# A gated linear recurrence on TensorE: two levels in one row of products, and half the query columns in the next four

## The chip, the cores and the metric

The kernel runs on one core of one Trainium2 chip. The metric is device microseconds of one execution. TensorE (PE in the profile; PEld is its weight load) multiplies a stationary operand of up to 128 columns with a streamed operand and writes to PSUM; VectorE (DVE) and ScalarE (ACT) do elementwise work; GpSimd (POOL) does small things here; SyncE (SP) issues the weight transfers.

## The reference

Two decoder layers on 256 tokens of width 1024, float32. A layer normalises x, projects it by `h @ w_in` into ten groups of 512 columns, runs three branches side by side, multiplies their outputs by silu(gate), projects by `w_out` and adds x:

- MoBA attention, 8 heads of 64 (with 256 tokens there is one block, so it is causal attention over the block);
- HGRN2, a gated linear recurrence, 4 heads with key and value width 128;
- attention to 256 memory tokens, 4 heads of 128.

The change is in the recurrence. For a head, with query q_t (after silu), key k_s, value v_s and a forget gate f_t per key channel, the reference computes, chunk by chunk,

```
scores[t, s] = sum_d q[t, d] * (f[s+1, d] * ... * f[t, d]) * k[s, d]     for s <= t
o[t] = sum_s scores[t, s] * v[s]
```

and then a per-head RMS norm of o.

## The kernel before, in words

**Projections.** The weights come in chunks of 128 x 1024. For each chunk ScalarE makes a rounded copy `wh` (L144, L147) and VectorE the remainder `wl` (L156, L159); TensorE multiplies them in three passes with the split activations (L196, `acc`; the output projection is L1051). These projections are most of TensorE's work. The chunks are loaded five ahead, `wh` is made three ahead and `wl` two ahead.

**The order.** The stream of projections is cut into slots of a few multiplies. In each slot the function `step` gives every active generator (one for each side job: the recurrence, a branch, a transposition) one turn; `yield n` means that the generator sits out n slots. So the side jobs' instructions are laid between the projections. PSUM has four side tiles (`sd`) beside the four accumulators; `room("sd")` waits for one to be free. After that a scheduler of the language orders each engine's instructions by its own simulated times; the recurrence's products go through `mm_row`, which keeps them in the program's order.

**The recurrence (g_hgrn, L711 to L808).** Q, K and F hold queries, keys and gates as [key channel 128, head 4 x token 256], 1024 columns. The products of gates are never formed for every pair (s, t). Instead there are levels m = 0, 1, 2, 4, ..., 64, then a last one over halves of 128:

- At level m the pairs are those whose s lies in an even run of m tokens and t in the odd run behind it (m = 0: s = t). By then each Q in an odd run has been multiplied by the gates from its run's start to t, and each K in an even run by the gates from behind s to its run's end, so a plain product K^T Q over key channels gives the scores of these pairs.
- For m below 32 (L729 to L733) TensorE computes, for each of the 32 blocks of 32 tokens (8 halves of heads i, 4 blocks j in each), the whole 32 x 32 product: 32 key columns are loaded, 32 query columns are streamed, and the result goes to partitions 32j of a side tile. Four blocks j use four column groups of the array. Only some of the 32 x 32 are pairs of the level; L756 copies these from PSUM into `hSd` under the mask `mk[:, j]`, [128, 8, 32] elements.
- Behind the products VectorE prepares the next level: L746 multiplies the odd runs of Q by a gate product, L747 the even runs of K, L750 makes the gate products of runs twice as long. At level 0 it is one product Q * F (L753) over all 1024 columns.
- Levels 32 and 64 (L735 to L740) use only the odd run's queries; ScalarE copies them into `hST` (L762). After level 16 four ScalarE copies (L767) put `hSd` on the diagonal of `hST`.
- Each level is two slots, products, two slots, elementwise work (`yield 2`, `yield 2`), then the next.
- Behind the levels come the product over halves (L773), the product of the scores with the values (L788, L790), the norm, and the transposition into the output's layout (L699).

One f32 product shows as two weight loads and two multiplies in the trace.

**Before it.** g_q (L639) makes Q = acc * sigmoid(acc) in two halves of 512 columns (L646) and starts g_hgrn when the second is issued. Q's buffer has the tag `hq0`, shared with a memory tile that is done by then.

Of the kernel before, what the change touches and what calls it, by code (L numbers as in the profile page):

```python
# [12 lines left out]
F32 = mybir.dt.float32  # L13
# [5 lines left out]
OP = mybir.AluOpType  # L19
# [26 lines left out]
def hymba_kernel(ctx: ExitStack, tc: tile.TileContext, x, mem, mem_t, positions, w_in, w_out, w_mem_kv,  # L46
                 gains, moba_g, out):
    nc = tc.nc
    cst = ctx.enter_context(tc.tile_pool(name="cst", bufs=1))
    sb = ctx.enter_context(tc.tile_pool(name="sb", bufs=1))  # L50
# [12 lines left out]
    def room(what, n=1):  # L63
        while held[what] + n > room_of[what]:
            yield
# [9 lines left out]
    def side_tile():  # L75
        held["sd"] += 1
        assert held["sd"] <= 4
        return psum.tile([128, 512], F32, name="sd", tag="sd", bufs=4)

    def rel(what="sd", n=1):  # L80
        held[what] -= n

    def small(name, n):
        return sb.tile([128, n], F32, name=name, tag=name, bufs=2)
# [81 lines left out]
    T = {}  # L166
# [10 lines left out]
    def spawn(gen, delay=1):  # L177
        active.append([delay, gen])
# [16 lines left out]
    def mm(o, a, b, s, e):  # L195
        nc.tensor.matmul(o, lhsT=a, rhs=b, start=s, stop=e)  # L196


    def mm_row(o, a, b):
        tc.keep_in_program_order(nc.tensor.matmul(o, lhsT=a, rhs=b, start=True, stop=True))  # L200
# [161 lines left out]
    hT = sb.tile([128, 8, 2, 256], F32R, name="hT")  # L362
# [59 lines left out]
    mk = cst.tile([128, 6, 32], U8, name="mk")  # L422
    hSd = cst.tile([128, 8, 32], F32, name="hSd")
# [5 lines left out]
    hST = sb.tile([128, 4, 2, 128], F32, name="hST")  # L429
# [102 lines left out]
    def heads(t, n):  # L532
        return t.rearrange("p (h d) -> p h d", h=n)

    def sumsq(dst, acc, n):
        sq = sb.tile([128, 512], F32, name="sq", tag="sq", bufs=2)
        nc.scalar.activation(sq, acc, AF.Square)
        nc.vector.tensor_reduce(dst, heads(sq, n), AX.X, OP.add)

    def rsq(name, ss, n, width):  # L540
        ms = small(name + "m", n)
        nc.vector.tensor_scalar(ms, ss, 1.0 / width, EPS, op0=OP.mult, op1=OP.add)
        r = small(name + "r", n)
        nc.gpsimd.tensor_tensor(r, ms, pw[:, :n], op=OP.pow)
        return r
# [93 lines left out]
    def g_q(l, h0, acc):  # L639
        cs = slice(h0 * 256, h0 * 256 + 512)  # L640
        if h0 == 0:
            T["Q"] = sb.tile([128, 1024], F32, name="hQ", tag="hq0", bufs=1)
        sg = sb.tile([128, 512], F32, name="sg", tag="sg", bufs=2)
        nc.scalar.activation(sg, acc, AF.Sigmoid)
        yield
        nc.vector.tensor_tensor(T["Q"][:, cs], acc, sg, op=OP.mult)  # L646
        if h0 == 2:
            spawn(g_hgrn(l))

# [45 lines left out]
    def y_transpose(l, t, gain):  # L695
        yield from room("sd")
        pt = side_tile()
        for j in range(4):
            nc.tensor.transpose(pt[:, j * 128:(j + 1) * 128], zh[:, t, j * 128:(j + 1) * 128], ident)  # L699
        p3 = heads(pt, 4)  # L700
        oh, ol = (a[:, :, t * 128:(t + 1) * 128] for a in y_tiles(H_))
        nc.scalar.activation(oh, p3, AF.Copy, scale=gain)
        nc.vector.scalar_tensor_tensor(ol, in0=p3, scalar=gain, in1=oh.bitcast(F32), op0=OP.mult, op1=OP.subtract)
        rel()
        yield
        if t == 1:
            for k in range(4):
                done.add(f"y{4 * H_ + k}_{l}")


    def g_hgrn(l):  # L711
        Q, K, F = T["Q"], T["K"], T["F"]
        T.pop(f"y{H_}", None)
        Q4, K4 = Q.rearrange("p (h s) -> p h s", h=4), K.rearrange("p (h s) -> p h s", h=4)
        yield

        St = hST.rearrange("p h t s -> p (h t) s")

        Tm = F
        m = 0
        while m < 128:
            yield 2
            yield from room("sd")
            g = side_tile()
            if m < 32:  # L729
                for i in range(8):  # L730
                    for j in range(4):
                        c = slice(i * 128 + j * 32, i * 128 + j * 32 + 32)
                        mm_row(g[j * 32:j * 32 + 32, i * 32:i * 32 + 32], K[:, c], Q[:, c])  # L733
            else:
                for a in range(0, 8, 2):  # L735
                    for q in range(0, 128, 2 * m):
                        for b in range(2):
                            c = (a + b) * 128 + q
                            mm_row(g[q + b * m:q + b * m + m, a // 2 * m:(a // 2 + 1) * m],
                                   K[:, c:c + m], Q[:, c + m:c + 2 * m])  # L740
            yield 2
            if m:
                n = 1024 // (2 * m)
                Qv, Kv = (a.rearrange("p (n two m) -> p n two m", two=2, m=m) for a in (Q, K))
                Tv = Tm.rearrange("p (n two) -> p n two", two=2)
                nc.vector.tensor_tensor(Qv[:, :, 1], Qv[:, :, 1], Tv[:, :, 0:1].to_broadcast([128, n, m]), op=OP.mult)  # L746
                nc.vector.tensor_tensor(Kv[:, :, 0], Kv[:, :, 0], Tv[:, :, 1:2].to_broadcast([128, n, m]), op=OP.mult)  # L747
                if m < 64:
                    T2 = sb.tile([128, n], F32, name=f"hT{m}", tag=f"hT{m}", bufs=1)
                    nc.vector.tensor_tensor(T2, Tv[:, :, 0], Tv[:, :, 1], op=OP.mult)  # L750
                    Tm = T2
            else:
                nc.vector.tensor_tensor(Q, Q, F, op=OP.mult)  # L753
            if m < 32:
                j = m.bit_length()
                nc.vector.copy_predicated(hSd, mk[:, j][:, None, :].to_broadcast([128, 8, 32]),  # L756
                                          g[:, 0:256].rearrange("p (a s) -> p a s", s=32))
            else:
                S2 = hST.rearrange("p h t s -> p (h t) s").rearrange("p (a b) s -> p a b s", b=2)
                for q in range(0, 128, 2 * m):  # L760
                    for b in range(2):
                        nc.scalar.copy(S2[q:q + m, :, b, q + m:q + 2 * m],  # L762
                                       g[q + b * m:q + b * m + m, 0:4 * m].rearrange("p (a s) -> p a s", s=m))
            rel()
            if m == 16:
                for q in range(0, 128, 32):
                    nc.scalar.copy(hST.rearrange("p h t s -> p (h t) s")[q:q + 32, :, q:q + 32], hSd[q:q + 32])  # L767
            m = 2 * m or 1
        yield 3
        yield from room("sd")  # L770
        g = side_tile()
        for h in range(4):
            mm(g[:, h * 128:(h + 1) * 128], K4[:, h, 0:128], Q4[:, h, 128:256], True, True)  # L773
        xc = sb.tile([128, 512], F32, name="hX", tag="hX", bufs=1)
        nc.scalar.copy(xc, g)
        rel()
        yield 2
        while f"ih{l}" not in done:
            yield
        ih = T["ih"]  # L780
        po = []
        ss = small("ssh", 8)
        for t in range(2):
            yield from room("sd")
            o = side_tile()
            for h in range(4):
                hs = slice(h * 128, (h + 1) * 128)
                mm(o[:, hs], hST[:, h, t], ih[:, t, hs], True, t == 0)  # L788
                if t == 1:
                    mm(o[:, hs], xc[:, hs], ih[:, 0, hs], False, True)  # L790
            po.append(o)
            sumsq(ss[:, t * 4:t * 4 + 4], o, 4)
            yield
        r = rsq("hg", ss, 8, 128)
        yield 3
        while f"z{H_}{l}" not in done:
            yield
        for t in range(2):
            for h in range(4):
                z = zh[:, t, h * 128:(h + 1) * 128]  # L800
                nc.vector.scalar_tensor_tensor(z, in0=po[t][:, h * 128:(h + 1) * 128],
                                               scalar=r[:, t * 4 + h:t * 4 + h + 1], in1=z,
                                               op0=OP.mult, op1=OP.mult)
            rel()
            yield
        yield 2
        for t in range(2):
            yield from y_transpose(l, t, gT[:, GR_O + l:GR_O + l + 1])  # L808
# [296 lines left out]
    for l in range(DEPTH):  # L1105
# [4 lines left out]
        for gen in (g_ih, lambda l, a: g_qk(l, 1, a), lambda l, a: g_qk(l, 0, a), g_zh, A_, M_, g_qm, g_va):  # L1110
            if gen in (A_, M_):
                group_a(hT, lambda h, a, br=gen: g_zt(l, br, h, a))
            else:
                acc = group_b(hTh, hTl)
# [52 lines left out]
```

## Time and profile before

| | |
|---|---|
| timed runs, median (lowest, highest) | 413.47 us (413.17, 413.51) |
| profiled execution, first to last instruction | 411.3 us |
| TensorE busy | 405.3 us (99%) |
| weight loads (overlap with multiplies) | 336.7 us (82%) |
| VectorE busy | 305.1 us (74%) |
| ScalarE busy | 261.2 us (64%) |
| GpSimd busy | 54.0 us (13%) |
| DMA over the span | 165 GB/s mean |
| granted TensorE clock | 1.000 |

The page gives no time of the profiled execution other than its span; the timed runs lie 2.2 us above it. Busy time is the union of an engine's instructions. A multiply's recorded length holds its way through the array, so neighbouring multiplies overlap, and what one of them costs the stream is the distance from its start to the next one's start. In the rows, `128*32` is the stationary operand's rows and columns, `128x32 f32` the streamed one's; "x64" is the number of records merged into the row.

### The profile page before, as it was taken

To read this page: it belongs to the slowest core of one execution; us is meant where nothing else is said; L and a number is where in the kernel's file an instruction comes from. 1 tells how busy PE (TensorE), PEld (TensorE's weight loads), DVE (VectorE), ACT (ScalarE), POOL (GpSimd) and SP (SyncE) were. 2 spreads that over 40 slices of the span, in tenths; PEclk is the share of its full clock that TensorE was granted. 3 is DMA by queue.
4 is the path that set the end of the run, shared out by engine and by line. 5 is a ranking of instruction groups with operands and counts; after the bars stand their busy time and mean duration, and the time that the engine had idled before them with its cause. 6 is when DMAs were issued, how large, how long until landed. Compare 5 with 4: busy or idle time off the path is not lost.

```text
span 411.3 us, 7610 instructions
## 1 busy us (share of the span) xinstructions
PE 405.3 (99%) x2940; PEld 336.7 (82%) x2940; DVE 305.1 (74%) x592; ACT 261.2 (64%) x431; POOL 54.0 (13%) x79
## 2 busy tenths in 40 slices
PE   8999999999999999999999999999999999999996
PEld 6788887878878888888878888878887888888885
DVE  4789886788778867776468689659888689568654
ACT  5867864444869985945356676444474999767430
POOL 2005105064000102000000020005500010200000
PEclk9999999999999999999999999999999999999999
DMA  7984566436341465344446555554545135643312
GB/s 273 411 297 131 182 204 206 155 125 224 117 155 55 147 194 170 102 155 153 153 155 205 179 180 168 190 178 169 168 134 177 53 102 180 216 153 117 107 49 102
DMA packets 19621, 67.76 MB, mean 165 GB/s; under 512 B 2432, under 2 KB 2816, under 8 KB 19584
## 3 DMA queue, kind: packets, MB, share of 16 engines
q1 hardware_dynamic: 19296, 67.12, 49.2%
q8 instruction: 23, 0.38, 0.4%
q10 hardware_dynamic: 288, 0.15, 0.1%
q14 instruction: 14, 0.11, 0.1%
HBM read 66.22 MB, written 1.05 MB: 164 GB/s over the span
## 4 chain that ended last, share of the span: by engine, by line
PE 92%; DMA 3%; DVE 2%; ACT 1%; issue 1%; SPq 0%; DVEq 0%
PE acc L196 61%; PE acc L1051 15%; PE sd L196 6%; PE sd L200 4%; DMA wr<-in_w_mem_kv_dram 3%; PE sd L915 1%; PE sd L852 1%; PE sd L1014 1%; DVE wl L159 1%; PE sd L403 1%; ACT wh L147 1%; PE sd L960 0%; PE sd L699 0%; PE sd L579 0%; DVE wl L156 0%
## 5 line engine op out<-in xcount | busy, mean ns | idle before, releaser
L156 DVE TENSOR_TENSOR wl<-wr,wh 128x1024 fp32r<-128x1024 f32 x104 | 127.0, 1224 | 45.3 <-ACT wh L144 45.1
L144 ACT CAST wh<-wr 128x1024 fp32r<-128x1024 f32 x104 | 109.1, 1052 | 69.1 <-PE acc L196 51.0
L196 PE MATMUL acc<-wh,hT 128*128 128x512 f32 x384 | 122.0, 394 | 0.0
L196 PE MATMUL acc<-hT,wh 128*128 128x512 f32 x256 | 91.4, 398 | 0.3 <-DVE vml L594 0.3
L196 PEld LDWEIGHTS acc<-wh,hT 128*128 128x128 f32 x384 | 71.6, 188 | 14.4
L196 PE MATMUL acc<-wl,hT 128*128 128x512 f32 x192 | 76.5, 399 | 0.0
L196 PE MATMUL acc<-hT,wl 128*128 128x256 f32 x256 | 72.3, 282 | 0.0
L196 PEld LDWEIGHTS acc<-hT,wh 128*128 128x128 f32 x256 | 48.0, 187 | 12.7 <-issue 1.3
L196 PEld LDWEIGHTS acc<-hT,wl 128*128 128x128 f32 x256 | 48.4, 189 | 0.9 <-issue 0.7
L196 PEld LDWEIGHTS acc<-wl,hT 128*128 128x128 f32 x192 | 36.1, 188 | 7.1
L1051 PE MATMUL acc<-wl,yh 128*128 128x512 f32 (+1 forms) x96 | 37.4, 389 | 0.0
L1051 PE MATMUL acc<-wh,yl 128*128 128x512 f32 (+1 forms) x96 | 37.1, 393 | 0.0
L1051 PE MATMUL acc<-wh,yh 128*128 128x512 f32 (+1 forms) x96 | 35.7, 392 | 0.0
L196 PE MATMUL acc<-wh,mTh 128*128 128x512 f32 x64 | 25.5, 399 | 1.1 <-ACT wh L147 0.6
L159 DVE SCALAR_TENSOR_TENSOR wl<-wr,gT,wh 128x1024 fp32r<-128x1024 f32 (+1 forms) x17 | 20.2, 1220 | 8.0 <-ACT wh L147 8.0
L147 ACT ACTIVATE wh<-wr,gT 128x1024 fp32r<-128x1024 f32 (+1 forms) x17 | 18.4, 1099 | 11.7 <-PE acc L1051 5.0
L196 PE MATMUL acc<-wh,mTl 128*128 128x512 f32 x64 | 25.0, 390 | 0.0
L820 POOL TENSOR_TENSOR rka<-msa,pw 128x8 f32<-128x8 f32 x4 | 14.2, 3562 | 55.3 <-DVE msa L819 55.3
L1051 PEld LDWEIGHTS acc<-wl,yh 128*128 128x128 f32 x96 | 18.0, 188 | 3.8
L1051 PEld LDWEIGHTS acc<-wh,yh 128*128 128x128 f32 x96 | 18.0, 188 | 3.7
L1051 PEld LDWEIGHTS acc<-wh,yl 128*128 128x128 f32 x96 | 17.9, 188 | 3.8
L196 PE MATMUL acc<-wl,mTh 128*128 128x512 f32 x64 | 20.8, 393 | 0.2 <-DVE wl L159 0.2
(208 smaller groups left out, 590.6 us busy)
## 6 DMA issues: line engine op xcount, KB each, us to landing
wr<-in_w_in_dram SPq DMA_DIRECT2D x80, 512.0 KB, 3.4
wr<-in_w_out_dram SPq DMA_DIRECT2D x24, 512.0 KB, 3.5
wr<-in_w_mem_kv_dram SPq DMA_DIRECT2D x15, 512.0 KB, 3.4
xs<-in_x_dram SPq DMA_DIRECT2D x2, 512.0 KB, 8.6
memr<-in_mem_dram SPq DMA_DIRECT2D x2, 512.0 KB, 6.4
out_dram<-xs SPq DMA_DIRECT2D x3, 256.0 KB, 2.0
mraw<-in_mem_t_dram SPq DMA_DIRECT2D x2, 256.0 KB, 5.1
wr<-in_w_mem_kv_dram SPq DMA_DIRECT2D x2, 256.0 KB, 4.6
```

The source lines that it names most:

```text
L144: nc.scalar.copy(whs[i], raws[i])
L147: nc.scalar.activation(whs[i][:, sl], raws[i][:, sl], AF.Copy, scale=gT[:, g:g + 1])
L156: nc.vector.tensor_tensor(wls[i], raws[i], whs[i].bitcast(F32), op=OP.subtract)
L159: nc.vector.scalar_tensor_tensor(wls[i][:, sl], in0=raws[i][:, sl], scalar=gT[:, g:g + 1], in1=whs[i][:, sl].bitcast(F32), op0=OP.mult, op ...
L196: nc.tensor.matmul(o, lhsT=a, rhs=b, start=s, stop=e)
L200: tc.keep_in_program_order(nc.tensor.matmul(o, lhsT=a, rhs=b, start=True, stop=True))
L403: ins = nc.tensor.transpose(pt[:, j * 256 + t * 128:j * 256 + (t + 1) * 128], xn[t][:, k * 128:(k + 1) * 128], ident)
L820: nc.gpsimd.tensor_tensor(r[:, t8], ms[:, t8], pw[:, :8], op=OP.pow)
L852: nc.tensor.transpose(pt[:, p * 128:(p + 1) * 128], kr[:, t, p * 128:(p + 1) * 128], ident)
L915: nc.tensor.transpose(pt[:, i * 128:(i + 1) * 128], P[:, i, bs], ident)
L1014: nc.tensor.transpose(pt[:, i * 256 + t * 128:i * 256 + (t + 1) * 128], P[:, t, i, b * 128:(b + 1) * 128], ident)
L1051: ins = nc.tensor.matmul(a, lhsT=y, rhs=wt[:, cs], start=n == (0 if to is None else nk - 2) and j == 0, stop=n == nk - 1 and j == 2)
```

## The change

Three things, all for blocks of 32 tokens; what is computed stays the same.

1. Q gets a wider tile, 32 blocks of 48 columns. The first 32 of a block hold the queries, the last 16 (`Q1`) hold the 16 odd queries already multiplied by their own gate. These are made by one VectorE product ahead of the first row. The first row of products then streams all 48 columns against the block's keys: columns 0 to 31 are level 0, columns 32 to 47 level 1. Two masked copies (`put`) take them into `hSd`. The loop starts at m = 1 and has seven rounds in place of eight.
2. At levels 2, 4, 8 and 16 only the odd runs' query columns, 16 of 32, are streamed, with a stride; the masked copies handle 128 in place of 256 elements.
3. The elementwise work follows: the product Q * F of all columns becomes one for the odd columns (into Q1, ahead of the first row) and one for the even ones (behind it); the odd columns of Q are then written from Q1 at level 1.

Levels 32 and 64 and the product over halves keep their shape and read Q with the new stride.

```diff
@@ g_q
-            T["Q"] = sb.tile([128, 1024], F32, name="hQ", tag="hq0", bufs=1)
+            T["Q"] = sb.tile([128, 32, 48], F32, name="hQ", tag="hq0", bufs=1)
...
-        nc.vector.tensor_tensor(T["Q"][:, cs], acc, sg, op=OP.mult)
+        nc.vector.tensor_tensor(T["Q"][:, h0 * 8:h0 * 8 + 16, 0:32], heads(acc, 16), heads(sg, 16), op=OP.mult)
@@ g_hgrn
-        Q, K, F = T["Q"], T["K"], T["F"]
+        QX, K, F = T["Q"], T["K"], T["F"]
...
+        Q, Q1 = QX[:, :, 0:32], QX[:, :, 32:48]
...
+        def odd(a, m):
+            return a.rearrange("p a (n two m) -> p a n two m", two=2, m=m)[:, :, :, 1]
...
+        def put(j, d, g, m):
+            mj = mk[:, j][:, None, :]
+            if m:
+                mj, d = odd(mj, m), odd(d, m)
+                g = g.rearrange("p a (n m) -> p a n m", m=m)
+            nc.vector.copy_predicated(d, mj.to_broadcast([128, 8] + list(g.shape)[2:]), g)
+
+        yield
+        F3 = F.rearrange("p (b s) -> p b s", s=32)
+        Q1v = Q1.rearrange("p b (n m) -> p b n m", m=1)
+        nc.vector.tensor_tensor(Q1v, odd(Q, 1), odd(F3, 1), op=OP.mult)
         Tm = F
-        m = 0
+        m = 1
         while m < 128:
             yield 2
...
             if m < 32:
+                w = 48 if m == 1 else 16
                 for i in range(8):
                     for j in range(4):
-                        c = slice(i * 128 + j * 32, i * 128 + j * 32 + 32)
-                        mm_row(g[j * 32:j * 32 + 32, i * 32:i * 32 + 32], K[:, c], Q[:, c])
+                        c = i * 4 + j
+                        mm_row(g[j * 32:j * 32 + 32, i * w:i * w + w], K[:, c * 32:c * 32 + 32],
+                               QX[:, c] if m == 1 else odd(Q[:, c:c + 1], m)[:, 0])
...
             yield 2
-            if m:
-                n = 1024 // (2 * m)
...
+            if m < 32:
+                Tb = Tm.rearrange("p (b n two) -> p b n two", b=32, two=2)
+                bc = [128, 32, 16 // m, m]
+                if m == 1:
+                    nc.vector.tensor_tensor(even(Q, 1), even(Q, 1), even(F3, 1), op=OP.mult)
+                nc.vector.tensor_tensor(odd(Q, m), Q1v if m == 1 else odd(Q, m), Tb[:, :, :, 0:1].to_broadcast(bc),
+                                        op=OP.mult)
             else:
-                nc.vector.tensor_tensor(Q, Q, F, op=OP.mult)
...
             if m < 32:
-                j = m.bit_length()
-                nc.vector.copy_predicated(hSd, mk[:, j][:, None, :].to_broadcast([128, 8, 32]),
-                                          g[:, 0:256].rearrange("p (a s) -> p a s", s=32))
+                gs = g[:, 0:8 * w].rearrange("p (a s) -> p a s", s=w)
+                if m == 1:
+                    put(0, hSd, gs[:, :, 0:32], 0)
+                put(m.bit_length(), hSd, gs[:, :, w - 16:], m)
...
-            m = 2 * m or 1
+            m *= 2
```

More of the change, by code (lines that the diff above doesn't have):

```diff
@@ L711, in g_hgrn, with even @@
     def g_hgrn(l):
-        Q, K, F = T["Q"], T["K"], T["F"]
+        QX, K, F = T["Q"], T["K"], T["F"]
         T.pop(f"y{H_}", None)
-        Q4, K4 = Q.rearrange("p (h s) -> p h s", h=4), K.rearrange("p (h s) -> p h s", h=4)
+        Q, Q1 = QX[:, :, 0:32], QX[:, :, 32:48]
+        K4 = K.rearrange("p (h s) -> p h s", h=4)
+        St = hST.rearrange("p h t s -> p (h t) s")
+        def odd(a, m):
+            return a.rearrange("p a (n two m) -> p a n two m", two=2, m=m)[:, :, :, 1]
+        def even(a, m):
+            return a.rearrange("p a (n two m) -> p a n two m", two=2, m=m)[:, :, :, 0]
+        def put(j, d, g, m):
[4 more added lines that the diff above has]
+            nc.vector.copy_predicated(d, mj.to_broadcast([128, 8] + list(g.shape)[2:]), g)
         yield
-        St = hST.rearrange("p h t s -> p (h t) s")
+        F3 = F.rearrange("p (b s) -> p b s", s=32)
+        Q1v = Q1.rearrange("p b (n m) -> p b n m", m=1)
+        nc.vector.tensor_tensor(Q1v, odd(Q, 1), odd(F3, 1), op=OP.mult)
         Tm = F
-        m = 0
+        m = 1
         while m < 128:
@@ L739, in g_hgrn @@
                             mm_row(g[q + b * m:q + b * m + m, a // 2 * m:(a // 2 + 1) * m],
-                                   K[:, c:c + m], Q[:, c + m:c + 2 * m])
+                                   K[:, c:c + m], Q[:, (c + m) // 32:(c + 2 * m) // 32])
             yield 2
-            if m:
-                n = 1024 // (2 * m)
[L744 to L751, printed above, removed]
-            else:
-                nc.vector.tensor_tensor(Q, Q, F, op=OP.mult)
+            n = 1024 // (2 * m)
@@ new lines, in g_hgrn @@
+            Kv = K.rearrange("p (n two m) -> p n two m", two=2, m=m)
+            Tv = Tm.rearrange("p (n two) -> p n two", two=2)
+            if m < 32:
[5 more added lines that the diff above has]
+                                        op=OP.mult)
+            else:
+                Qv = Q.rearrange("p (n two a) s -> p n two a s", two=2, a=m // 32)[:, :, 1]
+                nc.vector.tensor_tensor(Qv, Qv, Tv[:, :, 0:1][:, :, :, None].to_broadcast([128, n, m // 32, 32]),
+                                        op=OP.mult)
@@ L754, in g_hgrn @@
+            nc.vector.tensor_tensor(Kv[:, :, 0], Kv[:, :, 0], Tv[:, :, 1:2].to_broadcast([128, n, m]), op=OP.mult)
+            if m < 64:
+                T2 = sb.tile([128, n], F32, name=f"hT{m}", tag=f"hT{m}", bufs=1)
+                nc.vector.tensor_tensor(T2, Tv[:, :, 0], Tv[:, :, 1], op=OP.mult)
+                Tm = T2
             if m < 32:
-                j = m.bit_length()
-                nc.vector.copy_predicated(hSd, mk[:, j][:, None, :].to_broadcast([128, 8, 32]),
-                                          g[:, 0:256].rearrange("p (a s) -> p a s", s=32))
+                gs = g[:, 0:8 * w].rearrange("p (a s) -> p a s", s=w)
+                if m == 1:
+                    put(0, hSd, gs[:, :, 0:32], 0)
+                put(m.bit_length(), hSd, gs[:, :, w - 16:], m)
@@ L766, in g_hgrn @@
                 for q in range(0, 128, 32):
-                    nc.scalar.copy(hST.rearrange("p h t s -> p (h t) s")[q:q + 32, :, q:q + 32], hSd[q:q + 32])
-            m = 2 * m or 1
+                    nc.scalar.copy(St[q:q + 32, :, q:q + 32], hSd[q:q + 32])
+            m *= 2
         yield 3
@@ L772, in g_hgrn @@
         for h in range(4):
-            mm(g[:, h * 128:(h + 1) * 128], K4[:, h, 0:128], Q4[:, h, 128:256], True, True)
+            mm(g[:, h * 128:(h + 1) * 128], K4[:, h, 0:128], Q[:, h * 8 + 4:h * 8 + 8], True, True)
         xc = sb.tile([128, 512], F32, name="hX", tag="hX", bufs=1)
```

## The prediction, made before the change was run

> **What bounds the kernel now.** I read the page of the whole execution first (busy time, then the chain of waits), then the groups by line and shape for TensorE, and then the order of time around one level of the recurrence.
>
> ```profile
> span 411.3 us, 7610 instructions
> PE 405.3 (99%) x2940; PEld 336.7 (82%) x2940; DVE 305.1 (74%) x592; ACT 261.2 (64%) x431; POOL 54.0 (13%) x79
> ...
> PEclk9999999999999999999999999999999999999999
> ...
> PE 92%; DMA 3%; DVE 2%; ACT 1%; issue 1%; SPq 0%; DVEq 0%
> PE acc L196 61%; PE acc L1051 15%; PE sd L196 6%; PE sd L200 4%; DMA wr<-in_w_mem_kv_dram 3%; PE sd L915 1%; PE sd L852 1%; PE sd L1014 1%; DVE wl L159 1%; PE sd L403 1%; ACT wh L147 1%; PE sd L960 0%; PE sd L699 0%; PE sd L579 0%; DVE wl L156 0%
> ```
>
> TensorE is never idle to speak of, at full granted clock, and 92% of the chain that ended last is its own work. So a microsecond of TensorE work removed in the middle of a layer should come off the end, as long as no other engine becomes late; VectorE has a quarter of the span free. L200 (the small products of the recurrence, and of the MoBA scores) is 4% of the chain. That line by shape, multiplies and weight loads (columns: count | busy us, mean ns of one | idle before):
>
> ```profile
> L200 PE MATMUL sd<-hQ,hK 128*32 128x32 f32 x832 | 10.1, 199 | 0.0
> L200 PE MATMUL sd<-hQ,hK 128*64 128x64 f32 x32 | 1.4, 228 | 0.0
> ```
>
> ```profile
> L200 PEld LDWEIGHTS sd<-hQ,hK 128*32 128x32 f32 x832 | 8.5, 110 | 4.9 <-issue 4.2 <-PE acc L196 0.7
> L200 PEld LDWEIGHTS sd<-hQ,hK 128*64 128x64 f32 x32 | 1.1, 137 | 0.5 <-issue 0.5
> ```
>
> One f32 product is two recorded multiplies: 32 products of a level are 64 records, and 2 layers x (6 levels x 64 + 32 at level 32) = 832. What one level costs is not its busy time, but what it pushes back in the stream of projections. In order of time:
>
> ```profile
> 60.13 0.84 PE L196 MATMUL acc<-wh,hT 128*128 128x512 f32 x3
> 60.81 0.39 PE L196 MATMUL acc<-wl,hT 128*128 128x512 f32 x1
> ...
> 62.85 0.39 PE L196 MATMUL acc<-wh,hT 128*128 128x512 f32 x1
> 63.17 0.65 PEld L200 LDWEIGHTS sd<-hQ,hK 128*32 128x32 f32 x64 [0.35 <-issue]
> 63.17 0.76 PE L200 MATMUL sd<-hQ,hK 128*32 128x32 f32 x64
> ...
> 63.86 0.51 PE L196 MATMUL acc<-wh,hT 128*128 128x512 f32 x1
> ...
> 64.21 0.39 PE L196 MATMUL acc<-wl,hT 128*128 128x512 f32 x1
> ...
> 69.74 0.76 PE L200 MATMUL sd<-hQ,hK 128*32 128x32 f32 x64
> ...
> 263.30 0.76 PE L200 MATMUL sd<-hQ,hK 128*32 128x32 f32 x64
> ```
>
> Three projections start in 60.81 - 60.13 = 0.68 us, so one takes 0.227. From 62.85 to 64.21 there are two of them and one level: 1.36 - 2 x 0.227 = 0.91 us for a level of 64 multiplies. Inside it the first and last starts are 0.76 - 0.20 = 0.56 us apart, 8.9 ns per multiply; the other 0.91 - 0.57 = 0.34 us go at the two borders, where the array changes shape (62.85 to 63.17 where 0.227 is usual, and the 0.51 us of the first projection behind it).
>
> **What the change removes.** Six rows of 32 products (levels 0, 1, 2, 4, 8, 16) become five. One row and its two borders go: **-0.91 us per layer**. The second layer's level 0 stands at 263.30, 200.1 us behind the first's, with the same 0.76 us, so the price holds twice.
>
> **What it widens.** The first row streams 48 columns per product, not 32. The nearest rows are these two, of 32 and of 64 columns:
>
> ```profile
> 104.82 0.46 PE L200 MATMUL sd<-hQ,hK 128*32 128x32 f32 x32
> ...
> 111.06 0.69 PE L200 MATMUL sd<-hQ,hK 128*64 128x64 f32 x16
> 111.67 0.71 PE L200 MATMUL sd<-kT,qT 64*128 64x128 f32 x8
> 112.32 0.38 PE L196 MATMUL acc<-hT,wl 128*128 128x256 f32 x1
> ```
>
> 32 columns: (0.46 - 0.20)/31 = 8.4 ns per multiply with four column groups in turn. 64 columns: (0.69 - 0.23)/15 = 31 ns with two groups, so 15.3 ns if there were four. That is (15.3 - 8.9)/32 = 0.20 ns per column, or 3.2 ns for 16 columns, if it were all the streaming: +0.21 us for 64 multiplies of 48 columns. Below, the end is 0: the 64-column row also loads 64 weight columns, and its slope may be that of the loads. I take **+0.15 us**, nearer to the upper end, because 48 streamed columns are now more than the 32 loaded.
>
> **What it narrows.** Four rows (levels 2 to 16) stream 16 columns. By the same slope each could lose 0.21 us; the other end is 0. I take **0**: the weight loads stay at 32 columns, and their 64 starts lie (0.65 - 0.11)/63 = 8.6 ns apart, which is the multiplies' own pace. Shortening one of two partners that run in step doesn't shorten the step. The odd columns are read in short runs with a stride, which no row of before does for a streamed operand; a loss there is the slower rival below.
>
> [...]
>
> **What it moves.** A level takes four steps of the order (two before the products, two before the elementwise work), so every later row comes one row earlier. Level 64 then leaves the place at 111.06, where it shares a border with the MoBA scores (111.67 follows at once, without a projection between). If these scores then stand alone, a border comes back. One border pair is 0.34 us, so this lies between 0 and +0.34; I take **+0.15 us per layer**. The copies that end the recurrence come one row (some 6 us) earlier on ScalarE, that is rather before 125 than behind it, and ScalarE is freer there (stretch: length, PE, PEld, DVE, ACT busy):
>
> ```profile
> 62.00:100.00 38.00, 38.00 (x533) 30.45 (x532) 29.07 (x45) 16.60 (x20) 16.97 (x19) 1.00 0.54 175
> 100.00:125.00 25.00, 25.00 (x192) 20.43 (x189) 18.83 (x52) 19.30 (x41) 0.00 (x0) 1.00 0.40 136
> 125.00:167.00 42.00, 42.00 (x242) 36.06 (x241) 32.66 (x68) 34.32 (x62) 4.51 (x3) 1.00 0.47 151
> ```
>
> ```profile
> 102.10 1.65 ACT L767 COPY hST<-hSd 32x256 f32<-32x256 f32 x4 [1.13 <-DVE hSd L756]
> ```
>
> 19.3 of 25 us against 34.3 of 42: I put that move at nothing, hidden under the projections; with no idle time to take it, a weight cast behind it would come up to these 1.65 us later.
>
> **VectorE.** Groups by shape:
>
> ```profile
> L746 DVE TENSOR_TENSOR hQ<-hQ,hT 128x512 f32<-128x512 f32 x12 | 8.2, 687 | 0.0
> L756 DVE COPY_PREDICATED hSd<-mk,sd 128x256 f32<-128x256 uint8 x12 | 5.3, 440 | 0.0
> ...
> L753 DVE TENSOR_TENSOR hQ<-hQ,hF 128x1024 f32<-128x1024 f32 x2 | 2.5, 1225 | 1.6 <-PE sd L200 1.6
> ```
>
> 1024 elements take 1225 ns and 512 take 687, so 1.05 ns an element on 149 ns. The product of 1225 ns becomes two of 687 (odd ahead of the first row, even behind it): +149 ns per layer. Six masked copies of 440 ns become one of 256 elements (440) and five of 128 (440 - 134 = 306): 1970 for 2640, -670 ns. VectorE is relieved by about 0.5 us a layer, at no place where it sets the end: no gain. What counts is the one product that now stands *ahead* of the first row. VectorE before the first row of each layer:
>
> ```profile
> 58.73 0.69 DVE L646 TENSOR_TENSOR hQ<-as,sg 128x512 f32<-128x512 f32 x1 [0.67 <-ACT sg L644]
> 59.67 1.22 DVE L156 TENSOR_TENSOR wl<-wr,wh 128x1024 fp32r<-128x1024 f32 x1 [0.25 <-ACT wh L144]
> ...
> 62.16 1.31 DVE L156 TENSOR_TENSOR wl<-wr,wh 128x1024 fp32r<-128x1024 f32 x1 [0.77 <-ACT wh L144]
> 63.98 1.23 DVE L753 TENSOR_TENSOR hQ<-hQ,hF 128x1024 f32<-128x1024 f32 x1 [0.51 <-PE sd L200]
> 65.12 1.24 DVE L156 TENSOR_TENSOR wl<-wr,wh 128x1024 fp32r<-128x1024 f32 x1
> 66.28 0.44 DVE L756 COPY_PREDICATED hSd<-mk,sd 128x256 f32<-128x256 uint8 x1
> 67.99 1.23 DVE L156 TENSOR_TENSOR wl<-wr,wh 128x1024 fp32r<-128x1024 f32 x1 [1.27 <-ACT wh L144]
> ...
> 260.20 0.68 DVE L646 TENSOR_TENSOR hQ<-as,sg 128x512 f32<-128x512 f32 x1
> 261.82 1.23 DVE L156 TENSOR_TENSOR wl<-wr,wh 128x1024 fp32r<-128x1024 f32 x1 [0.94 <-ACT wh L144]
> ```
>
> The query is ready at 59.4 and 260.9; the rows start at 63.17 and 263.30. In the first layer the idle 0.77 us before 62.16, and in the second the 0.94 us before 261.82, each hold a product of 0.69, so I cost it at **0**. If that cover is gone and it queues behind the weight split (ending 263.05), it ends at 263.74, 0.44 us after the row wants it; behind the row wait the projections, for TensorE takes its queue in order. After the first row, even, odd, K and two masked copies are 3 x 0.69 + 0.44 + 0.31 = 2.8 us, beside two splits of 1.23, in the 5.8 us between 63.9 and the next row at 69.7: it fits with 0.5 us left, and the two copies aren't awaited.
>
> **Sum.** Per layer -0.91 + 0.15 + 0 + 0.15 = -0.61 us; twice, -1.2. The profiled execution's span goes from 411.3 to 410.1. The timed median, 413.47, is 2.2 us more than the span, a part outside it that the change doesn't touch; so **412.2 us**. The measurement can tell 0.2% (0.83 us) from no change; -1.2 is just beyond.
>
> **The rivals.**
> *Narrow rows pay after all.* If the pace is set by the streamed columns, each of the eight narrow rows loses 0.21 us and the wide one gains its full 0.21: per layer -0.91 + 0.21 - 0.84 + 0.15 = -1.39, in all 410.7. For it speaks the slope from 32 to 64 columns; against it, the loads' equal pace. Chance 0.13.
> *The gain is eaten on the way.* The first row waits 0.44 us for the odd product and the MoBA scores stand alone (0.34): -0.91 + 0.15 + 0.34 + 0.44 = +0.02 per layer, 413.5, no change. For it: TensorE has no other slack to hide a wait in; against it: both idle stretches are long enough. Chance 0.16.
> *Strided streaming is slow: slower than before.* The mechanism is the read of odd columns in runs of 2 to 16 of a 48-column block. If such a column costs fourfold, 16 cost as 64 do, 15.3 ns in place of 8.9: +0.41 us in each of eight rows, +3.3 - 1.2 = +2.1, that is 415.6. It decides (slower by 0.83) from (1.2 + 0.83)/8 = 0.25 us a row, 4 ns a multiply, about threefold per column. Nothing in the trace speaks for it; the elementwise products at all strides take the same 687 ns on VectorE, which speaks against it as far as another engine can. Chance 0.08. [...]
> *It doesn't do what it says*: the row is saved but the order is laid out anew and something else collides. Chance 0.03, either side.
>
> **How the numbers follow.** The forecast (411.7 to 412.7) has 0.60. Faster by over 0.2%, under 412.64: nearly all of it and the narrow-row case, 0.71. Within 0.2%: the eaten gain and the forecast's upper edge, 0.18. Slower: the strided case and part of the last, 0.11. The range, 410.8 to 413.5, takes in the forecast, half of the fast rival and nearly all of the eaten gain; strided reading and the far end of the fast one are left out.
>
> **What would show it.** Right: L200 records of hQ,hK fall from 864 to 736; a narrow row still spans about 0.56 us from first to last start, the wide one about 0.7; TensorE's busy time falls by 1.0 to 1.5 us. Wrong: a narrow row well under 0.5 us (the fast rival) or over 0.7 (strided); a gap of TensorE before the first row ended by VectorE (the eaten gain); new idle time before projections ended by a weight split.

## The result, and the profile after

| | before | after |
|---|---|---|
| timed runs, median (lowest, highest) | 413.38 us (413.17, 413.51) | 416.58 us (416.16, 417.25) |
| ratio, 95% interval | | 1.0077 (1.0064 to 1.0089) |
| profiled execution, first to last instruction | 411.3 us | 414.8 us |

The kernel became 0.77% **slower**; 412.2 us had been forecast, with a range up to 413.5. The page of the kernel after, where it answers to the lines shown of before:

```profile
span 414.8 us, 7362 instructions
PE 407.3 (98%) x2812; PEld 336.6 (81%) x2812; DVE 304.7 (73%) x594; ACT 261.4 (63%) x431; POOL 52.2 (13%) x79
...
PE 89%; DMA 3%; DVE 3%; ACT 3%; issue 1%; SPq 0%; DVEq 0%
```

There are 128 multiplies fewer, and TensorE is busy 2.0 us *longer*; its share of the chain that ended last went from 92% to 89%, and ScalarE's from 1% to 3%. The groups by line and shape, and the first two rows of the recurrence in order of time:

```profile
L200 PE MATMUL sd<-hQ,hK 128*32 128x16 f32 x512 | 5.9, 185 | 0.0
L200 PE MATMUL sd<-hQ,hK 128*32 128x48 f32 x128 | 1.8, 208 | 0.0
```

```profile
64.13 0.89 PE L200 MATMUL sd<-hQ,hK 128*32 128x48 f32 x64
...
71.97 0.74 PE L200 MATMUL sd<-hQ,hK 128*32 128x16 f32 x64
```

The recurrence itself did what it should. The records of hQ,hK fell from 864 to 736. A wide row takes 0.89 - 0.21 = 0.68 us from its first start to its last, a narrow one 0.74 - 0.185 = 0.555, where a row of 32 columns took 0.56 to 0.57. The loss lies elsewhere, and the MoBA scores (kT,qT) show it. All their groups in the first layer of the kernel after:

```profile
113.63 0.72 PE L200 MATMUL sd<-kT,qT 64*128 64x128 f32 x8
...
116.43 0.70 PE L200 MATMUL sd<-kT,qT 64*128 64x256 f32 x2
119.91 1.13 PE L200 MATMUL sd<-kT,qT 64*128 64x256 f32 x6
...
124.83 0.48 PE L200 MATMUL sd<-kT,qT 64*128 64x128 f32 x2
126.14 0.71 PE L200 MATMUL sd<-kT,qT 64*128 64x128 f32 x6
130.75 0.70 PE L200 MATMUL sd<-kT,qT 64*128 64x256 f32 x2
131.69 1.13 PE L200 MATMUL sd<-kT,qT 64*128 64x256 f32 x6
```

Before, the same 32 multiplies stood in five groups: the eight at 111.67, beside level 64, and these four, of which the last two follow at once on the product over halves (119.49) and on a product with the values (124.04):

```profile
114.72 0.70 PE L200 MATMUL sd<-kT,qT 64*128 64x256 f32 x2
116.13 1.13 PE L200 MATMUL sd<-kT,qT 64*128 64x256 f32 x6
...
120.47 0.72 PE L200 MATMUL sd<-kT,qT 64*128 64x128 f32 x8
...
125.03 1.13 PE L200 MATMUL sd<-kT,qT 64*128 64x256 f32 x8
```

So one eight was torn into 2 and 6; now there are seven groups, and three eights are torn. What a group costs the stream of projections can be read from the distances of starts around it:

```profile
124.62 0.28 PE L196 MATMUL acc<-hT,wl 128*128 128x256 f32 x1
124.83 0.48 PE L200 MATMUL sd<-kT,qT 64*128 64x128 f32 x2
125.25 0.50 PE L196 MATMUL acc<-hT,wh 128*128 128x512 f32 x1
125.58 0.28 PE L196 MATMUL acc<-hT,wl 128*128 128x256 f32 x1
...
125.93 0.28 PE L196 MATMUL acc<-hT,wl 128*128 128x256 f32 x1
126.14 0.71 PE L200 MATMUL sd<-kT,qT 64*128 64x128 f32 x6
126.78 0.51 PE L196 MATMUL acc<-hT,wh 128*128 128x512 f32 x1
127.12 0.28 PE L196 MATMUL acc<-hT,wl 128*128 128x256 f32 x1
```

A projection of 256 columns usually takes 0.12 us to the next start (125.58 to 125.70 in the same stream), one of 512 columns 0.23. So the group of two cost (125.25 - 124.62 - 0.12) + (125.58 - 125.25 - 0.23) = 0.61 us, and the group of six 0.73 + 0.11 = 0.84. An undivided group of eight costs 0.83 as well (shown with the seventh experiment below). Tearing two off eight thus costs about 0.6 us and saves nothing.

The second loss is a wait in layer 2. TensorE there, and ScalarE's queue ahead of it (eight exponentials follow the first table load; the first is shown):

```profile
351.61 1.14 PE L937 MATMUL sd<-ident,P 128*128 128x128 f32 x9
353.68 0.73 PE L196 MATMUL acc<-wh,hT 128*128 128x512 f32 x2 [0.93 <-ACT wh L144]
```

```profile
344.16 1.28 ACT L918 ACT_TABLE_LOAD   x1
345.45 0.49 ACT L918 ACTIVATE P<-P,nba,rq 128x128 f32<-128x128 f32 x1
...
349.72 1.03 ACT L144 CAST wh<-wr 128x1024 fp32r<-128x1024 f32 x1
350.77 1.28 ACT L674 ACT_TABLE_LOAD   x1
...
352.60 1.03 ACT L144 CAST wh<-wr 128x1024 fp32r<-128x1024 f32 x1
```

From 344.16 to 353.6 ScalarE finished one weight cast; the rest were two table loads, eight exponentials with their sums, and a sigmoid. The cast that ends at 353.6 is the one that TensorE waits for. Before, no projection waited for `wh` of this matrix; now it is 0.93 us, and the section of the trace in which it lies is 1.2 us longer.

The account, as time of TensorE beyond the usual steps of the projections, by sections of the trace: recurrence, scores and values (with the transpositions of `kr`, L852 before, that stand among them) took 16.89 us in each layer before, and 17.63 and 17.93 after, although the rows had become 0.88 cheaper. So 1.6 and 1.9 us were added elsewhere in the section. By group it is the scores in both layers, 1.6 us each (the sum stands with the first experiment). The other 0.3 us of layer 2 lie at level 64: that row costs 1.12 us there and 0.81 in layer 1, and the projection behind it, at 306.95, waits 0.18 us for VectorE (`tm`). The transpositions of P with the wait are 1.2 us more in layer 2. A further 0.66 us at 17 us from the start is a wait for the first weights, 0.76 us in all where the kernel before has 0.10. A second profile of the same kernel shows 0.35 there, and near 7 us an idle 1.65 us where the first has 0.41, so these waits belong to the execution and not to the change. Net of it: -1.8 + 3.5 + 1.2 = +2.9 of the 3.2 us that were timed.

### The profile page after: what moved, and what is told of

Same layout as the page of the kernel before. It is cut to its first block, busy times and chain, and to the rows that moved or that the text cites. A ratio compares the mean times of both kernels' runs of the same rounds, so it can differ in the third digit from the quotient of the medians.

```text
span 414.8 us, 7362 instructions
## 1 busy us (share of the span) xinstructions
PE 407.3 (98%) x2812; PEld 336.6 (81%) x2812; DVE 304.7 (73%) x594; ACT 261.4 (63%) x431; POOL 52.2 (13%) x79
## 4 chain that ended last, share of the span: by engine, by line
PE 89%; DMA 3%; DVE 3%; ACT 3%; issue 1%; SPq 0%; DVEq 0%
PE acc L196 59%; PE acc L1073 15%; PE sd L196 6%; PE sd L200 4%; DMA wr<-in_w_mem_kv_dram 3%; PE sd L937 1%; ACT wh L144 1%; PE sd L1036 1%; DVE wl L159 1%; PE sd L874 1%; PE sd L403 1%; ACT wh L147 1%; DVE xs L1107 0%; DVE wl L156 0%; PE sd L982 0%
## 5 line engine op out<-in xcount | busy, mean ns | idle before, releaser
L147 ACT ACTIVATE wh<-wr,gT 128x1024 fp32r<-128x1024 f32 (+1 forms) x17 | 18.5, 1100 | 12.0 <-PE acc L1073 4.9
L842 POOL TENSOR_TENSOR rka<-msa,pw 128x8 f32<-128x8 f32 x4 | 12.6, 3145 | 58.2 <-DVE msa L841 58.2
```

What stands on the lines that cost most here:

```text
L147: nc.scalar.activation(whs[i][:, sl], raws[i][:, sl], AF.Copy, scale=gT[:, g:g + 1])
L842: nc.gpsimd.tensor_tensor(r[:, t8], ms[:, t8], pw[:, :8], op=OP.pow)
```

## The experiments

The theory: the level that went takes its four turns with it, so all that follows in the recurrence (the halves, the values) comes four turns earlier relative to the MoBA scores, and these are torn by it; the columns have nothing to do with the loss. The rivals: the streamed columns or the elementwise work cost more than it seems; or it isn't the turns, but the order in which the language's scheduler lays the multiplies. Ratios are against the kernel before on the same chip, and counts of changes of array shape are counted over the trace's records of multiplies in order of time.

### The four turns given back at the front

```diff
         m = 1
+        yield 4
         while m < 128:
```

> The changed kernel, with the four turns that the dropped round took put back ahead of the first row of products, so that from the second row on everything stands at the turns of the kernel before. Theory A (the order): the loss comes from where the end of the recurrence now stands, among MoBA's score products, which are torn into more groups, each paying its borders; with the old turns the score products are in as many groups as before and only the saved row is left, some 0.85 us a layer: 411.7 us. Rival B (transfers and placement: the wider Q tile moves everything in SBUF, the first weights land later, weight casts come late): the order changes nothing, 415 to 416.6 us.

Measured: 412.37 us, ratio 0.9958 (0.9946 to 0.9970), that is -1.56 us. All the new arithmetic is kept, and the kernel is now faster than before. The profiled execution spans 410.7 us, and TensorE is busy 403.5, 1.8 us less than before. The span is only 0.6 us shorter because TensorE waits for its first weights longer in this execution: 1.48 us near 7 us and 0.32 near 18.5, where the profile of before has 0.60 and nothing. The same list of scores, with the recurrence's other products beside them:

```profile
110.90 0.69 PE L200 MATMUL sd<-hQ,hK 128*64 128x64 f32 x16
111.52 0.72 PE L200 MATMUL sd<-kT,qT 64*128 64x128 f32 x8
114.83 0.70 PE L200 MATMUL sd<-kT,qT 64*128 64x256 f32 x2
116.00 1.13 PE L200 MATMUL sd<-kT,qT 64*128 64x256 f32 x6
119.64 1.05 PE L196 MATMUL sd<-hQ,hK 128*128 128x128 f32 x8
120.62 0.71 PE L200 MATMUL sd<-kT,qT 64*128 64x128 f32 x8
124.20 1.05 PE L196 MATMUL sd<-ih,hST 128*128 128x128 f32 x8
125.18 1.14 PE L200 MATMUL sd<-kT,qT 64*128 64x256 f32 x8
```

These are the groups of before, 0.2 us off at most, level 64 beside the first of them again. TensorE's time beyond the projections differs from before by -0.88 us a layer, in the recurrence's rows, and by next to nothing in any other kind of small product. By group, with the cost worked out as above and a neighbour's own cost taken off, the scores of layer 1 come to 0.65 + 2.09 + 0.84 + 1.26 = 4.84 us here, and to 0.85 + 0.82 + 1.25 + 0.61 + 0.84 + 2.09 = 6.46 in the kernel after: 1.6 us for the same 32 multiplies.

### The same turns taken from the kernel before

Level 0 of the kernel before sits out no slots; its columns and products stay.

```diff
-            yield 2
+            if m:
+                yield 2
...
-            yield 2
+            if m:
+                yield 2
```

> The kernel before, all its products kept, but level 0 takes no turns of its own (the two waits of two turns are left out at m = 0), so that all that follows comes four turns earlier, as in the changed kernel. Theory A: the score products are torn apart here too, with nothing saved: about 0.6 us for each of some four more groups, plus waits, 415.5 to 417 us. Rival B: nothing of the change is in it, 413.4 us.

Measured: 420.49 us, ratio 1.0152 (1.0139 to 1.0166), a loss of 6.6 us without a single new column, and more than the 415.5 to 417 us expected. The scores stand in the same seven groups as in the kernel after (8, 2, 6, 2, 6, 2, 6, the first at 117.79 us and the last at 133.80). Projections wait 0.9 us for casts here as well, and 0.5 for splits. So the shift of turns by itself tears the scores. The loss is 3.4 us larger than that of the change, and the rows that the change saves account for 1.8 of it. That wait for splits accounts for 0.5, and the transpositions of `kr` in layer 2 for another 0.5 (2.40 us where the kernel after has 1.88), with a wait of 0.35 us for VectorE behind them. The rest was not located.

### The four turns given back behind the levels

```diff
-        yield 3
+        yield 7
```

> The changed kernel, with the four turns put back behind the last level, ahead of the product over halves: the rows of products stay a row earlier, only the tail (product over halves, products with the values, norm) is back at its old turns. Theory A, if it is the tail that tears the scores apart: 411.5 to 412.5 us. Theory A, if it is the rows of levels 32 and 64: 414 us or more. Rival B: 415 to 416.6 us.

Measured: 413.80 us, 0.9994 (0.9986 to 1.0003): no change from before, and between the two cases of theory A. The levels stay four turns early, only halves and values go back. Layer 1 is better than with the turns at the front (14.96 us where that has 16.01 in recurrence, scores and values), layer 2 loses it again. Where the turns are given back matters, and the two layers don't follow one rule.

### Six turns at the front

```diff
         m = 1
+        yield 6
         while m < 128:
```

> The changed kernel with six turns put ahead of the first row: the tail comes two turns later than in the kernel before. Theory A: what counts is how many groups the score products and the recurrence stand in; if the later tail lets more of them stand together, up to two groups of 0.6 us fewer than before, 410.6 to 411.7 us. Rival B: 415 to 416.6 us.

Measured: 413.23 us, 0.9984 (0.9975 to 0.9992), between the two forecasts. The array changes its shape 46 times here, as few as in any run, against 50 with four turns and 54 before, and the MoBA scores keep TensorE busy for 7.4 us, where they take 8.8 with four turns and 8.8 before. But TensorE waits near 139 and 339 us, 0.5 us for casts and 1.1 for splits in all: the gain is eaten by the second loss. Fewer borders alone don't make the faster kernel.

### TensorE's multiplies in the program's own order, before and after

`mm` gets the rule that `mm_row` has; the scheduler then may not reorder any multiply that goes through the two. The transpositions and the output projection (L1051) are issued otherwise and stay free.

```diff
     def mm(o, a, b, s, e):
-        nc.tensor.matmul(o, lhsT=a, rhs=b, start=s, stop=e)
+        tc.keep_in_program_order(nc.tensor.matmul(o, lhsT=a, rhs=b, start=s, stop=e))
```

The kernel before with this rule:

> The kernel before, with all side multiplies and the projections of w_in and the memory kept in the order in which the program writes them; the scheduler may no longer move them. It is the base for the next two. Where TensorE then has to wait for a late input it can't step past, this costs time by itself: 412 to 418 us; its own value decides nothing.

The kernel after with this rule:

> The changed kernel with the same rule. In the written order it has the score products in as many groups as the kernel before under that rule. Theory A (the loss of the change comes from the scheduler's new order, not from the turns nor from the products): faster than the kernel before under the same rule by the saved rows, 1.5 to 1.9 us. Rival D (the four turns themselves bring the tail to a bad place, whoever orders): not faster than it, or slower.

Measured: 423.26 us, 1.0232 (1.0217 to 1.0248), and 423.52 us, 1.0244 (1.0223 to 1.0266); the first lies above its 412 to 418 us. With the order fixed, the scores keep the same groups in both, and the rows save 0.91 us a layer; yet nothing is left of it. Weight loads of the kernel after under this rule, with the idle time before them:

```profile
L937 PEld LDWEIGHTS sd<-ident,P 128*128 128x128 f32 x48 | 5.5, 140 | 2.3 <-ACT PT L938 1.8
L699 PEld LDWEIGHTS sd<-ident,zh 128*128 128x128 f32 x16 | 2.1, 139 | 1.6 <-DVE zh L823 0.8
```

The same loads waited 0.5 and 0.2 us in the kernel before under this rule. The section of the transpositions grows from 4.43 to 5.89 us a layer: what TensorE saves early it waits for later, on ScalarE's copies of P and VectorE's zh. So the theory that only the scheduler's new order costs the gain **fell**. The four turns cost it in either case: as torn groups where the scheduler orders, as waits where it may not. The rule as such costs 2.3% and isn't a way out. A part of that is one wait early in both kernels, 4.0 us for VectorE's `kn` that ends near 46 us; the mean granted clock of the profiled execution is 0.991 in both, and 1.000 in the profile of before.

### The price of torn groups

On the fixed order of before, the MoBA unit gives up its turn once inside its loop over four products.

```diff
             for i in range(4):
+                if i == 1:
+                    yield
```

> The kernel before under the same rule, with one turn put between the second and the third of a MoBA unit's four score products, so that each group of four becomes two of two: six more groups, nothing else changed. It prices a torn group: theory A, two borders of 0.2 to 0.3 us each, so 2.4 to 3.6 us over the first of these three kernels. Rival (borders hide under the weight loads, tearing is free): within 0.5 us of it.

Measured: 427.08 us against 423.26, +3.8 us, a little above the 2.4 to 3.6 expected. First a whole group (the kernel before with fixed order), then half of it (this kernel):

```profile
119.86 0.28 PE L196 MATMUL acc<-hT,wl 128*128 128x256 f32 x1
120.06 0.72 PE L200 MATMUL sd<-kT,qT 64*128 64x128 f32 x8
120.71 0.50 PE L196 MATMUL acc<-hT,wh 128*128 128x512 f32 x1
121.04 0.28 PE L196 MATMUL acc<-hT,wl 128*128 128x256 f32 x1
```

```profile
120.54 0.28 PE L196 MATMUL acc<-hT,wl 128*128 128x256 f32 x1
120.75 0.49 PE L200 MATMUL sd<-kT,qT 64*128 64x128 f32 x4
121.17 0.50 PE L196 MATMUL acc<-hT,wh 128*128 128x512 f32 x1
121.50 0.28 PE L196 MATMUL acc<-hT,wl 128*128 128x256 f32 x1
```

Half a group costs (121.17 - 120.54 - 0.12) + (0.33 - 0.23) = 0.61 us, two halves 1.2; the whole one costs 0.85 - 0.12 + 0.10 = 0.83. Two of the eight pieces in a layer still touch, so there are three more groups; they take the scores from 4.2 to 5.8 us, 0.52 each. That is 3.1 of the 3.8 us, and the transpositions of P, 0.6 us a layer dearer here, more than cover the rest. A cut thus costs time by itself. Into equal halves it is 0.4 to 0.5 us; the two further cuts of the kernel after, into two and six, cost 0.6 (128 columns) and 0.8 (256 columns), and with 0.2 us for the border at level 64 these are its 1.6 us a layer.

### The values six turns later

In the kernel after, the `yield 2` behind the copy of the halves' result, ahead of the wait for `ih`:

```diff
         rel()
-        yield 2
+        yield 8
         while f"ih{l}" not in done:
```

> The changed kernel with six turns put between the product over halves and the products with the values: rows and product over halves stay early, only the products with the values and the norm come late. If the values' products are what tears the scores (each holds a side tile of PSUM until the norm is applied), most of the loss is gone: 412.5 to 414 us. If the rows and the product over halves do it: 415.5 us or more.

Measured: 417.20 us, 1.0092 (1.0067 to 1.0116), not faster than the kernel after. In layer 1 it mends the scores: four groups of eight, 4.23 us in all, and no values among them. So the values have a part in tearing them there. But layer 2 keeps two torn groups, with the values behind them all, and the casts become late in both; in layer 2 it is the split of such a cast that TensorE waits for, 1.37 us at 342. TensorE in layer 1, and the casts of ScalarE ahead of it:

```profile
141.69 0.74 PE L196 MATMUL acc<-wh,hT 128*128 128x512 f32 x2 [1.36 <-ACT wh L144]
142.95 0.51 PE L196 MATMUL acc<-wl,hT 128*128 128x512 f32 x1 [0.52 <-DVE wl L156]
```

```profile
131.30 1.03 ACT L144 CAST wh<-wr 128x1024 fp32r<-128x1024 f32 x1
...
138.78 1.28 ACT L674 ACT_TABLE_LOAD   x1
...
140.61 1.03 ACT L144 CAST wh<-wr 128x1024 fp32r<-128x1024 f32 x1
```

Between 131.30 and 140.61, 9.3 us, no weight is cast: a table load for eight exponentials, a square, a table load for the sigmoid and the sigmoid stand in one piece. In the kernel before, a cast is let in behind the fifth of these eight exponentials, and no two casts in this stretch begin more than 6.1 us apart.

### The kernel after, a second profile

> The changed kernel once more, with a second profile. The first profile of it shows TensorE waiting 0.8 us for weights at 17 us, the kernel before 0.1 us there. If that start belongs to the change, it is there again and the time is 416.6 us; if it differs from execution to execution, the wait changes and the median stays near 416.6 us, because the loss lies behind 100 us.

Measured: 416.77 us, 1.0072 (1.0055 to 1.0088). The torn groups and the wait for the cast in layer 2 come back (0.94 us where the first profile has 0.93); the wait near 17 us comes back at half its size (0.35 in place of 0.76). That is how the account above sets the order apart from the execution.

### Three other places of the turns

Four at the front and three more behind the levels (`yield 6` for `yield 3`):

> Four turns ahead of the first row and three more ahead of the product over halves: rows at the turns of the kernel before, the tail three turns later than there. If borders decide, it equals the first experiment (score products in as many groups), 0.42% under the kernel before, 411.7 us. If ScalarE decides (a burst of exponentials and table loads without a weight cast in it), any shift of the tail can bring a wait of 0.7 to 2 us a layer, 412.5 to 415 us.

Six at the front and one more behind:

> Six turns ahead of the first row and one ahead of the product over halves. Its score products stand in two groups fewer than before. If borders decide: some 1.2 us under the first experiment, 410.5 us. If ScalarE's bursts decide, it keeps the wait for weight casts that six turns alone had: 412.5 to 413.5 us.

None at the front and three more behind:

> The turns put back ahead of the product over halves alone, three of them (the third experiment had four). Its score products stand in seven groups, the fewest of all. If borders decide: 410 to 411 us. If ScalarE's bursts decide: like the third experiment, 413 to 415 us.

Measured: 419.10 us, 1.0129 (1.0114 to 1.0145); 417.72 us, 1.0089 (1.0064 to 1.0113); and 412.82 us, 0.9975 (0.9963 to 0.9986). All three lie outside both of their forecasts, so neither borders alone nor casts alone predict the time. The array changes its shape 50, 46 and 48 times in them. The two slow ones have no more borders than the two fastest kernels of this study; they have the second loss at its largest. The middle one, layer 1:

```profile
141.35 0.73 PE L196 MATMUL acc<-wh,hT 128*128 128x512 f32 x2 [1.11 <-ACT wh L144]
143.18 0.53 PE L196 MATMUL acc<-wl,hT 128*128 128x512 f32 x1 [1.09 <-DVE wl L156]
```

In the middle one, casts begin at 130.48 and then at 140.26 us; the pause is 9.8 us in both layers of both slow kernels. TensorE waits 2.1 to 2.2 us in each layer, and in one layer of each kernel its granted clock falls to 0.53 behind the waits (last section). The third has no such wait.

The length of the pause alone doesn't decide: the kernel after has one of 11.8 us from 317 to 329 and loses nothing there. Nor does the place alone. Pauses of 9.3 to 9.8 us that begin between 129 and 134 us, or 200 us later in layer 2, brought a wait in all four kernels that have them; one of 8.8 us from 329.35, in the kernel with four turns behind the levels, brought none; and the kernel after loses its 0.93 us to one of 8.4 us from 341.34. What makes the projections more or less patient wasn't tried.

## Why the prediction was wrong, step by step

- **The row removed, -0.91 us a layer: right.** With the turns given back, the rows that stand alone between projections cost 3.62 (four of them) where they cost 4.50 (five): -0.88 a layer, all parts of the change in it.
- **The wide row, +0.15: right in kind, a little high.** 0.68 against 0.57 is +0.11. Sixteen more columns do cost, and the upper end of the range that was given (0.21) did not come.
- **The narrow rows, 0: right.** They save 0.01 us each: rows of 16 and 32 columns cost nearly alike (0.555 and 0.567 us a row), one of 48 does not (0.68). The rival of fast narrow rows falls with them (it needed 0.21).
- **Strided streaming, the slower rival: wrong as a mechanism.** It needed 0.25 us more in each narrow row; the row at level 2, with runs of two columns, takes 0.555, and those of levels 4, 8 and 16, with longer runs, take the same. Most of the chance that had been given to a slower kernel (0.08 of 0.11) stood on this mechanism, so that it came out slower bears nothing of it out.
- **The product ahead of the first row, 0: right.** No row of the recurrence waits for it; the row at 64.13 shows no idle time before it. The rival of the eaten gain, which needed 0.44 us here, falls with it.
- **"What it moves", +0.15 us: this step failed.** It counted one lost border, of level 64 with the scores, between 0 and 0.34. That border did come back and cost 0.2 (0.85 for the first group alone, 0.65 beside level 64). But the move also brought the values in among the scores: one group of eight beside the halves became 2 + 6 (+0.6), and the last group of eight, before beside the values, became 2 + 6 as well (+0.8). Both of these prices are for the cuts: a place beside halves or values had saved nothing (1.73 us for halves and eight together, 0.89 and 0.84 apart). In all +1.6 us a layer, some ten times the term; layer 2 has 0.3 us more at level 64. The step looked at the row that moves and at its one neighbour, and not at all that moves behind it.
- **ScalarE's copies earlier, "at nothing": failed too.** ScalarE's load over 25 us was looked at, 19.3, and not what stands in its queue one after the other where the casts have least to spare. The copies didn't hurt. The exponentials did, in the new order that everything behind the scores got: 1.2 us in layer 2.
- **A microsecond of TensorE work removed "should come off the end, as long as no other engine becomes late".** The condition was not enough: another engine did become late, and TensorE's own work grew by the torn groups. Where everything else keeps its place the sentence holds: forecast without the term for moves, 2 x -0.76 = -1.52; measured with four turns given back, -1.56.
- **VectorE's relief, no gain: right, but the relief was half the size.** Its busy time fell by 0.4 us in all (305.1 to 304.7), not by 0.5 a layer, because a masked copy of 128 elements takes 353 ns and not 306; nothing followed from it.
- **"It doesn't do what it says", 0.03: this is what happened**, down to its words ("the row is saved but the order is laid out anew and something else collides"). It got too small a chance: in a kernel whose TensorE has no idle time, every turn that moves is a draw from the orders seen here, which run from -0.4% to +1.5% with the same or nearly the same work.

What stays open: why the scheduler cuts a group of eight into two and six when the values come near. The scores go through `mm_row` like the recurrence's rows, which keeps their order but lets projections in between; where `mm` has the rule too, no eight is cut, before or after, so the cuts are the scheduler's. Moving the values away took the cuts out of layer 1 and not out of layer 2, and one eight was cut before, with no values near; that it is the wait for a free side tile is only a guess. And why the pause of casts hurts at one place and not at another.

## What to carry to other kernels

Where side jobs are laid between a saturated stream by turns, removing a stage changes two things, its work and everybody's turn behind it; test them apart, by giving the turns back as an idle count (here one line, and 0.8% slower became 0.4% faster than before). Price a group of small multiplies by the starts around it, not by its busy time, and expect tearing a group to add two thirds of what the whole one cost (0.6 on 0.83 us, 0.8 on 1.26). Before calling a move on an engine free, list what stands in its queue without a break at the new place, and what the bound engine needs from it meanwhile.

## What the runs showed of the hardware

- Products of 32 loaded columns in four column groups start 8.8 ns apart for 16 streamed columns, 9.0 for 32 and 10.8 for 48 (0.555, 0.567 and 0.68 us over 63 steps). Reading the 16 with a stride, in runs of two, costs no more than in one run: the rows of levels 2, 4, 8 and 16, in runs of 2, 4, 8 and 16 columns, all last 0.74 us.
- Multiplies of 64 rows between projections of 128 rows cost 0.61 us for two, 0.61 for four, 0.84 for six and 0.83 for eight, of 128 columns each. From two to eight the price grows by 0.22 us only. Groups of the projections' own 128 rows and columns show no such first price: sixteen multiplies of the values cost 1.70 + 0.08 = 1.78 us (the kernel before, from 127.59) and the eight of the product over halves 0.89 (the kernel after, at 111.14), 0.11 for each.
- Loading ScalarE's table takes 1.28 us, and the next exponential starts right behind it (344.16 to 345.45); the copy ahead of it ends at 344.15.
- TensorE's granted clock fell to 0.53 in one of two layers with nearly the same waits. In the run with six turns at the front and one behind, over the same stall of casts in layer 1 and in layer 2:

```profile
143.40:147.00 3.60, 3.60 (x10) 2.78 (x10) 3.60 (x8) 0.97 (x2) 1.67 (x1) 0.53 0.50 181
...
346.40:350.00 3.60, 3.60 (x17) 2.94 (x17) 3.60 (x8) 1.99 (x3) 1.67 (x1) 1.00 0.77 199
```

The columns are length, the five engines' busy time with their counts, granted clock, share of DMA and GB/s. Behind the one stall the clock is 0.53 and ten multiplies run where seventeen run behind the other, about 1.6 us lost (seven of 0.23). No wait shown for TensorE there was longer than 1.11 us, but it was busy for only 3.2 of the 5.4 us before 143.4. It was busy for 3.21 of the 5.4 us before 346.4 as well, and behind those the clock stays at 1.00, so what makes it fall was not shown. In the run with four turns and three it is the other way round, with waits of 0.99 and 1.1 us in both layers: the clock stays at 1.00 in layer 1 (143.4 to 147.0) and is 0.53 in layer 2 (346.4 to 350.0).
